# A dispatch kernel bound by its transfers: the tile of 8 tokens moves from the end to the front, the next tile is loaded in four pieces, and the weights come in two loads

## The chip, the core and the metric

The kernel runs on one core of one Trainium2 chip. The metric is the device time of one execution in microseconds (us). Three runs of the kernel before gave 240.56, 240.60 and 241.61 us, a median of 240.6 us. One further execution was taken with the hardware profiler.

## What is computed

Each of 16 x 1024 tokens has a row of 512 float32 numbers and two weights. The output holds, for each token, its row times its first weight and its row times its second weight. The expert indices are an input, but nothing is done with them.

```python
batch, seq, hidden, n_experts = 16, 1024, 512, 8      # k = 2
x_expanded = x[:, :, np.newaxis, :].repeat(k, axis=2)
weights = expert_weights[..., np.newaxis]
return (x_expanded * weights).astype(np.float32)
```

So 33.6 MB of rows are read, 0.13 MB of weights are read, and 67.1 MB are written.

## The kernel before

The 16384 tokens are cut into six tiles over the 128 partitions. A tile of T tokens (per partition) takes T x 128 consecutive tokens, and partition p holds T consecutive ones of them, so that its part of the tile is one unbroken stretch of memory: T x 2 KB of input, T x 4 KB of output. `groups` (L32) gives the sizes: five tiles of 24, and one of 8 at the end. In this text x0 to x5 are the input tiles in the order in which they are loaded, x0.0 is the first piece of x0, and s0, s1, ... are the output stores in their order.

**Weights.** All weights of the core lie in one tile, `w_tile`. Three loads, all issued by SyncE (SP) at the start, fill it: those of the first tile (L53, 192 bytes for each partition), those of the four other tiles of 24 in one load (L54, 4 x 192 bytes for each partition), and those of the last tile (L58, 64 bytes for each partition).

**Input.** `load(i)` (L74) takes one of two input buffers (`x_pool`, 24 tokens each) and issues its loads on ScalarE's (ACT's) queue (L82). The first tile comes in six pieces of 4 tokens (`step`, L80), every other tile in one piece. `load(0)` and `load(1)` are issued at the start; `load(i + 2)` (L119) stands after the products of tile i and reuses its buffer, so it waits until VectorE (DVE) and ACT have read that tile.

**Products.** Each token has k = 2 products, numbered by the weight's column c. Where `c % 3 == 2`, ACT does the product (L100), otherwise DVE (L106): 85 and 171 of them. They are written to one of two output buffers of 12 tokens (`o_pool`, `TO = 12`).

**Output.** After each 12 tokens, or at the tile's end, SP issues one store (L115) of that buffer: ten stores of 12 tokens (6144 KB) and one last store of 8 tokens (4096 KB). A buffer is written again when its store has landed. SP's queue (q1 in the profile) thus carries the three weight loads and then the eleven stores, in this order; ACT's queue (q10) carries the input loads. Nothing but the Python order and the waits on buffers and tiles sets the order of the work.

Of the kernel before, what the change touches and what calls it, by code (L numbers as in the profile page):

```python
# [1 line left out]

# [4 lines left out]


@with_exitstack
def kernel(  # L10
    ctx: ExitStack,
    tc: tile.TileContext,
    x: bass.AP,
    expert_indices: bass.AP,
    expert_weights: bass.AP,
    out: bass.AP,
):
    nc = tc.nc

    batch, seq, hidden = x.shape  # L20
    k = expert_weights.shape[-1]
    P = nc.NUM_PARTITIONS
    ntok = batch * seq
    assert ntok % P == 0
    A_TOTAL = ntok // P

    f32 = mybir.dt.float32
    row = k * hidden
    TX = 24
    TO = 12  # L30

    groups = [[24], [24], [24], [24], [24], [8]]  # L32
    assert sum(sum(g) for g in groups) == A_TOTAL

    xf = x.rearrange("b s h -> (b s) h")
    of = out.rearrange("b s k h -> (b s) (k h)")
    wf = expert_weights.rearrange("b s k -> (b s) k")

    w_pool = ctx.enter_context(tc.tile_pool(name="w_pool", bufs=1))
    x_pool = ctx.enter_context(tc.tile_pool(name="x_pool", bufs=2))  # L40
    o_pool = ctx.enter_context(tc.tile_pool(name="o_pool", bufs=2))

    w_tile = w_pool.tile([P, A_TOTAL * k], f32)

    def rows(of_all, done, T):
        return of_all[done * P : (done + T) * P, :].rearrange(
            "(p a) n -> p (a n)", a=T
        )

    T0 = sum(groups[0])  # L50
    G = len([g for g in groups[1:] if sum(g) == T0])
    head = (1 + G) * T0
    nc.sync.dma_start(out=w_tile[:, : T0 * k], in_=rows(wf, 0, T0))  # L53
    nc.sync.dma_start(  # L54
        out=w_tile[:, T0 * k : head * k].rearrange("p (g n) -> p g n", g=G),
        in_=wf[T0 * P : head * P, :].rearrange("(g p a) n -> p g (a n)", g=G, p=P),
    )
    nc.sync.dma_start(  # L58
        out=w_tile[:, head * k :], in_=rows(wf, head, A_TOTAL - head)
    )  # L60

    tiles = []
    done = 0
    for group in groups:
        T = sum(group)
        a0 = 0
        for n in group:
            tiles.append((done, T, a0, n))
            a0 += n
        done += T  # L70

    loaded = []

    def load(i):  # L74
        if i >= len(tiles):
            return
        done, T, a0, n = tiles[i]
        x_tile = x_pool.tile([P, TX * hidden], f32)
        src = rows(xf, done, T)
        step = TX // 6 if i == 0 else n  # L80
        for at in range(0, n, step):
            nc.scalar.dma_start(  # L82
                out=x_tile[:, at * hidden : (at + step) * hidden],
                in_=src[:, (a0 + at) * hidden : (a0 + at + step) * hidden],
            )
        loaded.append(x_tile)

    for i in range(2):
        load(i)
    for i, (done, T, a0, n) in enumerate(tiles):  # L90
        x_tile = loaded[i]
        outr = rows(of, done, T)
        for t in range(n):
            if t % TO == 0:
                o_tile = o_pool.tile([P, TO * row], f32)
            for kk in range(k):
                c = (done + a0 + t) * k + kk
                o = t % TO * row + kk * hidden
                if c % 3 == 2:
                    nc.scalar.mul(  # L100
                        out=o_tile[:, o : o + hidden],
                        in_=x_tile[:, t * hidden : (t + 1) * hidden],
                        mul=w_tile[:, c : c + 1],
                    )
                    continue
                nc.vector.tensor_scalar(  # L106
                    out=o_tile[:, o : o + hidden],
                    in0=x_tile[:, t * hidden : (t + 1) * hidden],
                    scalar1=w_tile[:, c : c + 1],
                    scalar2=None,  # L110
                    op0=mybir.AluOpType.mult,
                )
            if (t + 1) % TO == 0 or t + 1 == n:
                at = t // TO * TO
                nc.sync.dma_start(  # L115
                    out=outr[:, (a0 + at) * row : (a0 + t + 1) * row],
                    in_=o_tile[:, : (t + 1 - at) * row],
                )
        load(i + 2)  # L119

# [1 line left out]
_INS = ['x', 'expert_indices', 'expert_weights']  # L122
_OUTS = [((16, 1024, 2, 512), 'float32')]


# [23 lines left out]
```

## Time and profile before

| | before |
|---|---|
| median of three runs (lowest to highest) | 240.6 us (240.56 to 241.61) |
| the profiled execution | 240.62 us, with a span of 238.9 us |
| around the span | 1.7 us |
| DVE busy | 69.0 us, 171 products of 480 ns |
| ACT busy | 54.9 us, 85 products of 709 ns and one table load of 1283 ns |
| moved | 100.81 MB in 3986 packets, mean 422 GB/s |

The profiled execution took 240.62 us, as long as the median of the runs. The span goes from the first to the last thing that the profiler records, and 1.7 us lie around it. The core's transfers run on 16 DMA engines. A packet is what one engine moves in one go; here one packet is one partition's part of a transfer, so each large transfer is 128 packets, 8 on each engine. "DMA share" in a row is the mean busy share of the 16 engines in that stretch (it can be over 1.00 in a short stretch, since packets are counted where they start).

### The profile page before, as it was taken

What the parts mean: (1) busy time and instruction counts of PE and PEld (TensorE: products, weight loads), DVE (VectorE), ACT (ScalarE), POOL (GpSimd) and SP (SyncE); (2) the same over time, 40 slices, a digit from 0 to 9 for tenths busy, and PEclk for the clock granted to TensorE, in tenths of its full rate; (3) what the DMA queues carried; (4) which work ended last, traced back from release to release, by engine and by line L of the source; (5) the groups of instructions that cost most, each with busy time, mean ns of one, the idle gap of its engine ahead of it and who ended that gap; (6) DMA issues with size and microseconds to landing.
All of it is one profiled execution on the core that took longest, in us unless ns stands there. A gap on an engine that the chain in (4) does not pass through costs nothing.

```text
span 238.9 us, 364 instructions
## 1 busy us (share of the span) xinstructions
DVE 69.0 (29%) x171; ACT 54.9 (23%) x86; POOL 0.2 (0%) x4
## 2 busy tenths in 40 slices
DVE  0890300004609100190063037003706406415000
ACT  0870300004308000170071034003406106213000
POOL 0000000000000000000000000000000000000000
DMA  6999999999999999999999999999989899999994
GB/s 244 420 443 395 495 395 395 494 428 395 428 494 395 413 494 411 395 446 469 403 411 502 395 420 453 436 411 428 469 379 496 381 428 469 436 411 428 436 439 197
DMA packets 3986, 100.81 MB, mean 422 GB/s; under 512 B 1168, under 2 KB 1168, under 8 KB 1168
## 3 DMA queue, kind: packets, MB, share of 16 engines
q1 hardware_dynamic: 2400, 67.24, 65.2%
q10 hardware_dynamic: 1584, 33.56, 33.1%
q14 instruction: 2, 0.02, 0.0%
HBM read 33.69 MB, written 67.11 MB: 422 GB/s over the span
## 4 chain that ended last, share of the span: by engine, by line
DMA 66%; DVE 13%; another core or an unknown queue 11%; issue 0%; DVEq 0%; SPq 0%
DMA out_dram<-o_tile 54%; DVE o_tile L106 13%; DMA x_tile<-in_x_dram 11%; DVEq L144 0%; DVEq L106 0%; SPq L115 0%
## 5 line engine op out<-in xcount | busy, mean ns | idle before, releaser
L106 DVE TENSOR_SCALAR o_tile<-x_tile,w_tile 128x512 f32<-128x512 f32 x171 | 69.0, 480 | 149.3 <-DMA out_dram<-o_tile 105.3
L100 ACT ACTIVATE o_tile<-x_tile,w_tile 128x512 f32<-128x512 f32 x85 | 53.6, 709 | 155.5 <-DMA out_dram<-o_tile 116.8
L100 ACT ACT_TABLE_LOAD x1 | 1.3, 1283 | 6.7 <-DMA x_tile<-in_x_dram 6.7
L133 POOL MEMSET const-bfloat16-1.0<- 128x1 bf16 x1 | 0.1, 101 | 0.0
L133 POOL MEMSET const-uint8-127<- 128x1 uint8 x1 | 0.1, 101 | 0.0
L133 POOL MEMSET const-float32-0.0<- 128x1 f32 x1 | 0.1, 98 | 0.2 <-issue 0.2
L133 POOL MEMSET const-float32-1.0<- 128x1 f32 x1 | 0.1, 98 | 0.0
## 6 DMA issues: line engine op xcount, KB each, us to landing
out_dram<-o_tile SPq DMA_DIRECT2D x10, 6144.0 KB, 33.6
x_tile<-in_x_dram ACTq DMA_DIRECT2D x4, 6144.0 KB, 43.9
x_tile<-in_x_dram ACTq DMA_DIRECT2D x6, 1024.0 KB, 10.6
out_dram<-o_tile SPq DMA_DIRECT2D x1, 4096.0 KB, 19.5
x_tile<-in_x_dram ACTq DMA_DIRECT2D x1, 2048.0 KB, 24.0
w_tile<-in_expert_weights_dram SPq DMA_DIRECT2D x1, 96.0 KB, 11.1
w_tile<-in_expert_weights_dram SPq DMA_DIRECT2D x1, 24.0 KB, 2.9
w_tile<-in_expert_weights_dram SPq DMA_DIRECT2D x1, 8.0 KB, 13.2
```

The costliest lines, as they stand in the source:

```text
L100: nc.scalar.mul(out=o_tile[:, o : o + hidden], in_=x_tile[:, t * hidden : (t + 1) * hidden], mul=w_tile[:, c : c + 1],)
L106: nc.vector.tensor_scalar(out=o_tile[:, o : o + hidden], in0=x_tile[:, t * hidden : (t + 1) * hidden], scalar1=w_tile[:, c : c + 1], scala ...
L133: nc = _bacc.Bacc("TRN2", target_bir_lowering=False, num_devices=1)
```

## The change

The tile of 8 tokens becomes the first tile, and is loaded in two pieces of 4 tokens. The tile after it (24 tokens) is loaded in four pieces of 6 tokens, and the four others in one piece as before. Each tile's pieces in and out now stand in one list, `plan`. The stores are one of 8 tokens, then ten of 12. With the odd tile in front, the weights of the other five tiles fit one load, so SP issues two weight loads: 64 bytes for each partition, then 5 x 192 bytes.

The core of the diff (the rest writes the same loops in another form: `product` holds the two ways of a product, and the `c % 3` split stays):

```diff
-    TX = 24
-    TO = 12
-    groups = [[24], [24], [24], [24], [24], [8]]
+    plan = [(8, [4, 4], [8]), (24, [6, 6, 6, 6], [12, 12])]
+    plan += [(24, [24], [12, 12])] * 4
...
-    T0 = sum(groups[0])
-    G = len([g for g in groups[1:] if sum(g) == T0])
-    head = (1 + G) * T0
+    T0, T1 = plan[0][0], plan[1][0]
+    G = len(plan) - 1
     nc.sync.dma_start(out=w_tile[:, : T0 * k], in_=rows(wf, 0, T0))
     nc.sync.dma_start(
-        out=w_tile[:, T0 * k : head * k].rearrange("p (g n) -> p g n", g=G),
-        in_=wf[T0 * P : head * P, :].rearrange("(g p a) n -> p g (a n)", g=G, p=P),
-    )
-    nc.sync.dma_start(
-        out=w_tile[:, head * k :], in_=rows(wf, head, A_TOTAL - head)
+        out=w_tile[:, T0 * k :].rearrange("p (g n) -> p g n", g=G),
+        in_=wf[T0 * P :, :].rearrange("(g p a) n -> p g (a n)", g=G, p=P),
     )
...
-        step = TX // 6 if i == 0 else n
-        for at in range(0, n, step):
+        for lo, hi in spans(pieces):
             nc.scalar.dma_start(
-                out=x_tile[:, at * hidden : (at + step) * hidden],
-                in_=src[:, (a0 + at) * hidden : (a0 + at + step) * hidden],
+                out=x_tile[:, lo * hidden : hi * hidden],
+                in_=src[:, lo * hidden : hi * hidden],
             )
...
+    for i, (T, _, outs) in enumerate(plan):
+        dst = rows(of, starts[i], T)
+        for lo, hi in spans(outs):
+            o_tile = o_pool.tile([P, TO * row], f32)
...
+            nc.sync.dma_start(
+                out=dst[:, lo * row : hi * row], in_=o_tile[:, : (hi - lo) * row]
+            )
         load(i + 2)
```

More of the change, by code (lines that the diff above doesn't have):

```diff
@@ L28 @@
     row = k * hidden
-    TX = 24
-    TO = 12
-    groups = [[24], [24], [24], [24], [24], [8]]
-    assert sum(sum(g) for g in groups) == A_TOTAL
+    plan = [(8, [4, 4], [8]), (24, [6, 6, 6, 6], [12, 12])]
+    plan += [(24, [24], [12, 12])] * 4
+    assert sum(T for T, _, _ in plan) == A_TOTAL
+    assert all(sum(i) == T and sum(o) == T for T, i, o in plan)
+    TX = max(T for T, _, _ in plan)
+    TO = max(n for _, _, o in plan for n in o)
     xf = x.rearrange("b s h -> (b s) h")
@@ L48, in rows @@
         )
-    T0 = sum(groups[0])
-    G = len([g for g in groups[1:] if sum(g) == T0])
-    head = (1 + G) * T0
+    T0, T1 = plan[0][0], plan[1][0]
+    G = len(plan) - 1
+    assert all(T == T1 for T, _, _ in plan[1:])
     nc.sync.dma_start(out=w_tile[:, : T0 * k], in_=rows(wf, 0, T0))
     nc.sync.dma_start(
-        out=w_tile[:, T0 * k : head * k].rearrange("p (g n) -> p g n", g=G),
-        in_=wf[T0 * P : head * P, :].rearrange("(g p a) n -> p g (a n)", g=G, p=P),
-    )
-    nc.sync.dma_start(
-        out=w_tile[:, head * k :], in_=rows(wf, head, A_TOTAL - head)
-    )
@@ L62, with spans @@
[L62 to L70, printed above, removed]
+        out=w_tile[:, T0 * k :].rearrange("p (g n) -> p g n", g=G),
+        in_=wf[T0 * P :, :].rearrange("(g p a) n -> p g (a n)", g=G, p=P),
+    )
+    def spans(sizes):
+        at = 0
+        for n in sizes:
+            yield at, at + n
+            at += n
+    starts = [lo for lo, _ in spans([T for T, _, _ in plan])]
@@ L72 @@
     loaded = []
     def load(i):
-        if i >= len(tiles):
+        if i >= len(plan):
             return
-        done, T, a0, n = tiles[i]
+        T, pieces, _ = plan[i]
         x_tile = x_pool.tile([P, TX * hidden], f32)
-        src = rows(xf, done, T)
-        step = TX // 6 if i == 0 else n
-        for at in range(0, n, step):
+        src = rows(xf, starts[i], T)
+        for lo, hi in spans(pieces):
             nc.scalar.dma_start(
-                out=x_tile[:, at * hidden : (at + step) * hidden],
-                in_=src[:, (a0 + at) * hidden : (a0 + at + step) * hidden],
+                out=x_tile[:, lo * hidden : hi * hidden],
+                in_=src[:, lo * hidden : hi * hidden],
@@ L85, in load @@
             )
         loaded.append(x_tile)
[L88 to L103, printed above, removed]
-                    )
[L105 to L118, printed above, removed]
@@ new lines, in product @@
+    def product(o_tile, o, x_tile, t, c):
+        if c % 3 == 2:
+            nc.scalar.mul(
+                out=o_tile[:, o : o + hidden],
+                in_=x_tile[:, t * hidden : (t + 1) * hidden],
+                mul=w_tile[:, c : c + 1],
+            )
+        else:
+            nc.vector.tensor_scalar(
+                out=o_tile[:, o : o + hidden],
+                in0=x_tile[:, t * hidden : (t + 1) * hidden],
+                scalar1=w_tile[:, c : c + 1],
+                scalar2=None,
+                op0=mybir.AluOpType.mult,
+            )
@@ new lines @@
+    load(0)
+    load(1)
+    for i, (T, _, outs) in enumerate(plan):
+        dst = rows(of, starts[i], T)
+        for lo, hi in spans(outs):
+            o_tile = o_pool.tile([P, TO * row], f32)
+            for t in range(lo, hi):
+                for kk in range(k):
+                    product(
+                        o_tile,
+                        (t - lo) * row + kk * hidden,
+                        loaded[i],
+                        t,
+                        (starts[i] + t) * k + kk,
+                    )
+            nc.sync.dma_start(
+                out=dst[:, lo * row : hi * row], in_=o_tile[:, : (hi - lo) * row]
+            )
```

## The prediction

> **What bounds the kernel now.** I read the page's slices and queues first. "DMA" is the busy share of the 16 DMA engines in tenths, in 40 slices of 6.0 us; below it is what they moved.
>
> ```profile
> DMA  6999999999999999999999999999989899999994
> GB/s 244 420 443 395 495 395 395 494 428 395 428 494 395 413 494 411 395 446 469 403 411 502 395 420 453 436 411 428 469 379 496 381 428 469 436 411 428 436 439 197
> ...
> q1 hardware_dynamic: 2400, 67.24, 65.2%
> q10 hardware_dynamic: 1584, 33.56, 33.1%
> ```
>
> The engines are full in all slices but the first and the last: 65.2% + 33.1% = 98.3% of 16 engines' span. DVE (29%) and ACT (23%) are idle mostly because they wait for transfers. So I cut the span into stretches (columns: DVE, ACT and POOL busy, clock, DMA share, GB/s):
>
> ```profile
> 3.00:14.00 11.00, 6.82 (x17) 6.61 (x10) 0.00 (x0) 1.00 1.02 416
> 14.00:16.90 2.90, 2.88 (x8) 1.75 (x4) 0.00 (x0) 1.00 1.03 362
> 16.90:40.00 23.10, 3.51 (x9) 3.26 (x6) 0.00 (x0) 1.00 1.01 432
> 40.00:120.00 80.00, 19.27 (x48) 15.03 (x24) 0.00 (x0) 1.00 1.00 434
> 150.00:193.00 43.00, 12.85 (x32) 10.02 (x16) 0.00 (x0) 1.00 1.00 432
> 193.00:235.00 42.00, 10.87 (x27) 8.18 (x13) 0.00 (x0) 1.00 0.99 430
> 235.00:238.90 3.90, 0.00 (x0) 0.00 (x0) 0.00 (x0) 1.00 0.24 101
> ```
>
> From 40 to 120 us the rate is 434 GB/s, whether loads run beside stores or, after 193 us, stores run alone (430). All 100.81 MB at 434 would be 232.3 us; the span has 6.6 us more. By rows: the start to 3.0 us (about 0.25 MB moved there) loses 2.4; the stretch with 8 KB load packets, 3 to 14 us at 416, loses 11 x (1 - 416/434) = 0.46; the 2.9 us in which the first store joins lose 2.9 x (1 - 362/434) = 0.48; the last 3.9 us at 101 GB/s lose 3.0; the rest is 0.3. By the trace's packet records the 16 engines stop between 235.8 and 237.6 us, on average at 236.4, and 1.3 us follow the last packet. That is all a new order of transfers could win.
>
> The start in order of time:
>
> ```profile
> 5.85 2.46 DVE L106 TENSOR_SCALAR o_tile<-x_tile,w_tile 128x512 f32<-128x512 f32 x6 [5.85 <-DMA x_tile<-in_x_dram]
> 6.70 1.28 ACT L100 ACT_TABLE_LOAD   x1 [6.70 <-DMA x_tile<-in_x_dram]
> 8.64 2.07 DVE L106 TENSOR_SCALAR o_tile<-x_tile,w_tile 128x512 f32<-128x512 f32 x5 [0.33 <-DMA x_tile<-in_x_dram]
> 11.23 2.07 DVE L106 TENSOR_SCALAR o_tile<-x_tile,w_tile 128x512 f32<-128x512 f32 x5 [0.52 <-DMA x_tile<-in_x_dram]
> 13.38 17.16 SPq L115 DMA_DIRECT2D out_dram<-o_tile  x2
> ```
>
> A piece of 1024 KB lands every 2.6 us, and the first store is issued at 13.38. In the packet records its first packet moves at 17.0; the loads issued beside running stores at 127.86 and 171.63 first move at 131.6 and 175.4. So 3.6 to 3.8 us pass from issue to first packet on a busy core.
>
> **The change part by part.**
>
> *Fewer, larger packets.* From the packet records 8 KB takes 0.309 us, 16 KB 0.611, 48 KB 1.815; 12 KB lies at about 0.46. Loads in small pieces were 768 x 0.309 + 128 x 0.611 = 315.5 us of engine time and become 256 x 0.309 + 512 x 0.46 = 314.6: 0.9 over 16 engines, -0.06 us. Bytes, 171 + 85 products and the store packets (1280 of 48 KB, 128 of 32 KB) stay.
>
> *Earlier first store.* x0 is complete with its second piece at 8.64. Of its 16 products DVE has 11 (6 before 8.64, 5 after, 2.07 us), ACT 5 (the table load no longer stands behind seven load issues; three products of 0.71 us after 8.64). So s0 is issued at about 10.8 instead of 13.38. This is worth nothing by itself: the engines are full with loads until then, and the same bytes are still to move.
>
> *Weights.* The 64-byte load takes the place of the 192-byte one in front and lands well before 5.85 (before: 2.9 us after issue). The second has 640 small packets, as many as L54 and L58 had together; these had landed at 1.63 + 13.2 = 14.8, L54 alone (512 packets) at 1.16 + 11.1 = 12.3. So 12.3 to 14.8. s0 stands behind it on SP's queue: its first packet at about 14.5 (10.8 + 3.7, the same). SP issues one load less (0.5 us, hidden). Zero.
>
> ```profile
> w_tile<-in_expert_weights_dram SPq DMA_DIRECT2D x1, 96.0 KB, 11.1
> w_tile<-in_expert_weights_dram SPq DMA_DIRECT2D x1, 24.0 KB, 2.9
> w_tile<-in_expert_weights_dram SPq DMA_DIRECT2D x1, 8.0 KB, 13.2
> ```
>
> The Trainium skill (DMA: Bandwidth & Descriptors, "Anatomy of one DMA — SWDGE (gpsimd) path") gives each transfer a fixed cost of about 2.0 us, stated for the gpsimd path. With 23 transfers in place of 25 it would make 4.0 us less, 236.6, if none of it were hidden; the 8.0 KB row, which lands while the engines are full, shows that it is hidden here.
>
> *New wait on ACT's queue.* As the changed kernel is built, ACT's sixth product (the second tile's first) stands ahead of the load of x2 and waits for x1.0 and the second weights; x2's load is queued behind it, and the DMA engines wait for that. x1.0 lands at 8.64 + 1.5 x 2.6 = 12.5, the weights by 14.8, so x2 starts to move by 14.8 + 0.8 (that product) + 3.8 (issue to first packet) = 19.4. The cover is x1, which alone lasts to 8.64 + 6 x 2.6 = 24.2, and s0's 4096 KB (9.7 us at 434): together 33.9. Without s0 it would still be 4.8 us. Zero; past 33.9 each us costs one.
>
> *Does SP's queue run dry?* With loads behind it this loses no engine time, but a store queue that starts again may cost a dip like the 0.48. The queues alternate packet by packet, each engine 8 packets a transfer. From 14.5 s0 and x1 (0.46 + 1.21 us a pair) take 13.4 us, so s0 ends at 27.9. x1.1 had 2 to 3 packets left at 14.5 and lands by about 18.5; 8 DVE products more, s1 issued at 22, moving by 25.7, before s0 is done. s1 then runs beside x1.2 and x1.3 (0.46 + 1.82 a pair) to about 46; x1.3 lands at 47, 3.3 us of products, s2 issued at 51, moving at 54.5. So SP's queue is empty once more, from 46 to 54.5, beside x2's 48 KB packets. No row of before has a store start beside those. Bounds: 0, by the load queue that starts again at 131.6 and 175.4 without a visible dip (432 in 150 to 193), and 0.48. I take 0.2, nearer to the first, since the packet sizes are those.
>
> *End.* After the last load only stores run, each waiting for a buffer: landing to next issue 6.5 us (16 DVE products of 6.43) and 3.7 to its first packet, 10.2, against 14.5 for the other buffer's 6144 KB at 434. Cover 4.3 us, as now. As no small tile is left, the store-only stretch begins earlier; I estimate some 23 us earlier, and 430 against 432 makes 0.1. The engines' stops, 1.25 us from mean to last, may be closer or wider: -1.2 to +0.6, taken as 0, since every engine has the same packets.
>
> *Sum:* 238.9 - 0.06 + 0.2 + 0.1 = 239.1 of span, plus 1.7: 240.8. The profiled execution (240.62) equals the median, so nothing is added.
>
> **Rivals.**
>
> *Slower: the store queue starts afresh several times.* If s0 moves already at 12.5, x1.1 has 6 to 7 packets left, lands at 23.8, and s1 moves only at 31, after s0 has ended at 25.9; s2 as above, and s3 too if x2 lands over 2.6 us later than I have it. Three starts at 0.48 are 1.44: 242.1; with the deeper start of small packets, 0.63 by the packet records, 242.5. It decides when s0's first packet is ahead of about 13.5 and the price holds beside large packets. For it: the 362 row. Against: no dip at 131.6 or 175.4.
>
> *Faster: the joining loss goes.* If s0 joins beside 12 KB packets without the 362 row (-0.48), half of the 416 loss goes (-0.23) and the engines stop half as far apart (-0.6), the span is 237.6: 239.3. For it: the loss sits where packets are smallest. Against: three parts must all come.
>
> *It does not do what it says:* s0 waits behind 640 weight packets, its first packet is at 17 as before, and nothing moves: 240.6.
>
> **How the numbers follow.** Within 0.5% is about what a measurement of this kernel can tell from no change (1.2 us, 239.4 to 241.8). My forecast has 0.60, its own range 239.7 to 241.7; the idle rival 0.05; both are "same": 0.65. The restarts have 0.21, all slower; the joining loss 0.14, faster. The range takes in both rivals' prices, 239.3 to 242.5, leaving out about 0.15.
>
> **What would show it.** First store issued near 10.8; second weights landing at 12.3 to 14.8; DMA share at 1.0 from 3 us to the end; a start of s2 near 54 beside a rate that stays at 430 or more. Wrong would be: a slice below 9 in the middle, a stretch below 400 after 20 us, or a start above 3 us to full rate.

## The result, and the profile after

The changed kernel took 242.02 us (median of 22 runs, 240.81 to 246.77), the kernel before 240.66 (22 runs, 240.53 to 241.61): a ratio of 1.0062 (95% interval 1.0048 to 1.0075), so it is slower by 0.6%. Its runs also scatter by 6 us (3.3 without the highest), where those of before lie within 1.1. The profiled execution took 242.59 us with a span of 240.8, somewhat above the median. (The ratios in this document leave out runs more than 1.5% above the fastest of their kernel; where a kernel's runs fall into two groups, that leaves out the upper one, and the text gives both.)

The page's slices and queues after, to be laid beside those of before:

```profile
DMA  6999999999999999999999999999999999999993
GB/s 223 424 400 461 441 437 441 412 416 351 449 465 392 442 465 400 433 474 400 416 475 416 408 482 416 400 490 408 400 490 416 400 474 433 400 457 441 408 441 147
...
q1 hardware_dynamic: 2384, 67.24, 64.8%
q10 hardware_dynamic: 1440, 33.56, 33.2%
```

The engines are as full as before: 98.0% of the span against 98.3%. But the tenth slice moved only 351 GB/s with its DMA digit at 9. The stretches say where (same columns as before: DVE, ACT, POOL, clock, DMA share, GB/s):

```profile
3.00:14.00 11.00, 4.54 (x11) 4.57 (x6) 0.00 (x0) 1.00 1.02 415
14.00:17.00 3.00, 0.00 (x0) 0.00 (x0) 0.00 (x0) 1.00 1.07 398
17.00:48.00 31.00, 9.77 (x24) 7.68 (x12) 0.00 (x0) 1.00 1.01 434
52.00:57.00 5.00, 0.15 (x1) 0.00 (x0) 0.00 (x0) 1.00 0.99 334
57.00:120.00 63.00, 17.09 (x43) 14.30 (x23) 0.00 (x0) 1.00 1.00 432
120.00:235.00 115.00, 34.32 (x86) 25.79 (x42) 0.00 (x0) 1.00 1.01 436
```

From 52 to 57 us the share is 0.99 and the rate 334: the engines are not idle, their packets take longer. Measured against the 434 GB/s of before, the loss is 5 x (1 - 334/434) = 1.15 us. In the packet records a 48 KB packet takes 1.815 us; 11 of 1792 took over 1.9 us before, together 0.21 us for each engine, and 34 after, 1.35 us.

By the packet records the profiled spans differ by 1.87 us in this way: the engines start 0.22 later on average (2.57 against 2.35), their slow packets cost 0.94 more in sum over the load and store packets (2.28 against 1.34 us an engine), the last engine stops 1.52 instead of 1.19 us after the mean, and 1.67 instead of 1.30 us follow the last packet. 0.22 + 0.94 + 0.33 + 0.37 = 1.86. (The records do not name the engine; packets are put in a row by one's end and the next's start.)

Of the 1.35 us, 1.08 lie between 52 and 56 us: 18 load packets of x2, of which sixteen, as many as there are engines, are under way at once near 55.6 us. After 60 us the packets over 1.9 us cost only 0.03 us an engine, against 0.17 in the kernel before. So in this run it is mainly one delay that all engines share. How far apart the engines are shows in another record: each transfer closes with one packet of 4 bytes for each engine. At the last five stores the first and the last of these packets lie 2.4 to 2.6 us apart, against 1.8 to 1.9 before.

The start and the middle in order of time:

```profile
17.20 3.26 DVE L91 TENSOR_SCALAR o_tile<-x_tile,w_tile 128x512 f32<-128x512 f32 x8 [6.08 <-DMA w_tile<-in_expert_weights_dram]
17.25 0.33 ACTq L77 DMA_DIRECT2D x_tile<-in_x_dram  x1
21.45 3.26 DVE L91 TENSOR_SCALAR o_tile<-x_tile,w_tile 128x512 f32<-128x512 f32 x8 [1.00 <-DMA x_tile<-in_x_dram]
35.48 3.26 DVE L91 TENSOR_SCALAR o_tile<-x_tile,w_tile 128x512 f32<-128x512 f32 x8 [10.77 <-DMA x_tile<-in_x_dram]
48.90 3.26 DVE L91 TENSOR_SCALAR o_tile<-x_tile,w_tile 128x512 f32<-128x512 f32 x8 [10.16 <-DMA x_tile<-in_x_dram]
```

The four pieces of x1 release DVE at 17.2 (held by the weights), 21.45, 35.48 and 48.90. s0 was issued at 11.20, s1 at 24.77, s2 at 52.22. In the packet records s0 first moves at 14.7 and ends at 30.2, s1 ends at 48.5, and s2 first moves at 56.8: SP's queue is empty from 48.5 to 56.8, and the shared delay lies just ahead of its new start.

### The profile page after: what moved, and what is told of

It is laid out like the page before. It is cut to its first block, busy times and chain, and to the rows that moved or that the text cites. A ratio compares the mean times of both kernels' runs of the same rounds, so it can differ in the third digit from the quotient of the medians.

```text
span 240.8 us, 366 instructions
## 1 busy us (share of the span) xinstructions
DVE 69.0 (29%) x171; ACT 54.9 (23%) x86; POOL 0.2 (0%) x4
## 4 chain that ended last, share of the span: by engine, by line
DMA 76%; DVE 12%; ACTq 1%; issue 0%; DVEq 0%; SPq 0%
DMA out_dram<-o_tile 58%; DMA x_tile<-in_x_dram 19%; DVE o_tile L91 12%; ACTq L77 1%; DVEq L142 0%; DVEq L91 0%; SPq L114 0%
## 6 DMA issues: line engine op xcount, KB each, us to landing
x_tile<-in_x_dram ACTq DMA_DIRECT2D x4, 1536.0 KB, 25.8
```

## The experiments

Three theories stood against each other at first. A: the new start of the empty store queue costs the time. B: the front costs it (the 64-byte weights first, one load of 640 small packets). C: the end costs it (a last store of 12 tokens). A fourth was added after the first runs (the pieces of 6, 6 and 12, the uncut tile, the smaller last store, and the kernel before with its first tile in pieces of 6). D: the second tile's small load packets, run beside stores, bring DMA engines out of step with each other (some finish their part of a transfer later than the others), and these then lose time. All kernels were timed against the kernel before, whose median was 240.58 to 240.67 us each time.

**Cutting the second tile differently.**

```diff
-    plan = [(8, [4, 4], [8]), (24, [6, 6, 6, 6], [12, 12])]
+    plan = [(8, [4, 4], [8]), (24, [6, 6, 12], [12, 12])]
```

> The changed kernel with the second tile loaded in three pieces of 6, 6 and 12 tokens instead of four of 6. Theory A (the store queue runs empty and its new start beside loads costs about 1.1 us of every DMA engine): the last piece now has 8 packets of 24 KB an engine in place of 16 of 12 KB, needs fewer turns beside the first two stores and lands before 40 us; the third store is issued near 43 us, before the second has ended near 48, so the queue does not run empty: 240.6 to 241.2 us, and no stretch below 400 GB/s after 20 us. Theory B (the front: the 64-byte weights first and 640 small packets ahead of the first store) and theory C (the end: the last store is 12 tokens instead of 8 and the engines stop further apart): nothing of theirs is touched, 242.0 us within 0.4.

Measured: 252.36 us (250.64 to 255.03), ratio 1.0477 (1.0436 to 1.0517). All three theories missed. The store queue is never empty between the first and the third store (s1 first moves at 31.1 while s0 ends at 32.9, s2 at 60.2 while s1 ends at 62.0), as theory A wanted it, and yet the kernel loses 12 us. Its stretches:

```profile
57.00:104.00 47.00, 8.10 (x21) 6.79 (x11) 0.00 (x0) 1.00 0.99 413
104.00:106.00 2.00, 2.00 (x6) 2.00 (x5) 0.00 (x0) 1.00 0.91 393
106.00:108.00 2.00, 2.00 (x6) 1.23 (x3) 0.00 (x0) 1.00 0.23 98
108.00:120.00 12.00, 0.75 (x2) 0.00 (x0) 0.00 (x0) 1.00 0.93 344
```

Here 176 of the 1792 packets of 48 KB are slow, 5.84 us for each engine. In the packet records three engines are slow again and again, about every 4 us, by 0.3 to 1.2 us at a time, from 32 to 113 us; the others far less often. A store has landed only when its last engine is done: the 4-byte packets of s2 show thirteen engines done by 90.0 us and three at 100.1 to 101.7, and DVE goes on at 102.3. So the products of the next stores wait for the laggards, and at 106 us the other engines have nothing left: share 0.23. Not all of the 5.84 us is theirs. Some 3.2 of it lie from 108 to 120 and from 156 to 164 us, where up to 15 and 13 slow packets are under way at once. At the end most engines stop at 245.1, the last at 251.6.

```diff
-    plan = [(8, [4, 4], [8]), (24, [6, 6, 6, 6], [12, 12])]
+    plan = [(8, [4, 4], [8]), (24, [24], [12, 12])]
```

> The changed kernel with the second tile loaded in one piece of 24 tokens. Theory A (new start of an empty store queue): the first store (8 packets of 32 KB an engine) alternates with 48 KB load packets and lasts to about 39 us; the second tile lands near 29, the second store is issued near 36 and the third near 42, so the queue has at most a short gap before the second store: 240.6 to 241.4 us. Theory B (front) and theory C (end): 242.0 us within 0.4.

Measured: 240.81 us (240.03 to 242.06), ratio 1.0009 (0.9994 to 1.0024). Undoing the four pieces alone gives the time back. The tile in front, the two weight loads and the end are all still there, so B and C fall. A expected it, and D, formed later, fits it as well: the 640 weight packets take until 24 us here (the last 128 from 8 us on, one for each load packet), s0 first moves at 22.9, and x1 has by then all but landed (23.9). A delay that engines share is there in this kernel too, just ahead of s0: thirteen load packets are slow at once at 21.3 us. It falls into the first of these stretches:

```profile
20.00:24.00 4.00, 0.00 (x0) 0.00 (x0) 0.00 (x0) 1.00 0.90 334
24.00:60.00 36.00, 12.85 (x32) 10.02 (x16) 0.00 (x0) 1.00 1.00 431
60.00:235.00 175.00, 51.39 (x128) 40.09 (x64) 0.00 (x0) 1.00 1.01 435
```

The edit also moves s0 behind x1, so by itself it does not tell the pieces from the pieces beside stores. In the kernel before, the uncut x1 (25.8 to 54.9 us) runs beside the first two stores.

```diff
-    plan = [(8, [4, 4], [8]), (24, [6, 6, 6, 6], [12, 12])]
+    plan = [(8, [4, 4], [8]), (24, [4] * 6, [12, 12])]
```

> The changed kernel with the second tile loaded in six pieces of 4 tokens (8 KB packets, those of the kernel before) instead of four of 6. The last piece lands near 48 us again and the store queue is empty from about 44 to 56 us. Theory A: 242.0 us within 0.5. Theory D, with 12 KB packets as the cause: 240.6 to 241.2 us.

Measured: 242.86 us (241.08 to 243.47), ratio 1.0074 (1.0051 to 1.0098). So 12 KB as a size is not special. The median lies above the ranges of both theories (A's ends at 242.5), and A's mechanism was not there: in the profiled run s1 ended at 54.7 and s2 first moved at 52.8, so the queue was not empty, against my arithmetic.

```diff
-    plan = [(8, [4, 4], [8]), (24, [6, 6, 6, 6], [12, 12])]
+    plan = [(8, [4, 4], [8]), (24, [12, 12], [12, 12])]
```

> The changed kernel with the second tile loaded in two pieces of 12 tokens (24 KB packets). The second piece lands near 35 us and the third store is issued near 42, before the second ends, so the store queue stays filled. Theory A: 240.6 to 241.2 us. Theory D, if it is the 24 KB packets beside stores that put engines out of step in the run with pieces of 6, 6 and 12 (252.4 us): well above 242 us.

Measured: median 241.25 us, ratio 1.0023 (1.0010 to 1.0035); nine of eleven runs lie from 240.69 to 242.06, two at 252.55 and 252.56. The median is just above A's range. D's "well above 242" came out in two runs only, which took as long as those with pieces of 6, 6 and 12.

**Keeping the store queue filled, with the pieces as they are.**

```diff
-    plan = [(8, [4, 4], [8]), (24, [6, 6, 6, 6], [12, 12])]
+    plan = [(8, [4, 4], [8]), (24, [6, 6, 6, 6], [12, 6, 6])]
```

> The changed kernel with the second tile stored in pieces of 12, 6 and 6 tokens instead of 12 and 12; its loads stay in four pieces of 6. The third store then needs only the third piece (landed at 35.4 us in the changed kernel's trace) and is issued near 39 us, before the second store ends at 48.5, so the store queue does not run empty. Theory A (an empty store queue pays about 1.1 us of all engines when it starts again): 240.6 to 241.2 us. Theory D (some DMA engines fall behind the others after 12 KB load packets have run beside stores, and the stores wait for the slowest engine): unchanged, 242.0 us within 0.5.

Measured: 242.09 us (241.53 to 244.01), ratio 1.0074 (1.0050 to 1.0099). The third store first moves at 46.5, before the second ends at 48.1. The queue is not empty, and nothing is won in the median, so A falls. The slow packets are there all the same (52 over 1.9 us, 1.21 us an engine; 14 load packets at once near 53.7 us), though the stretch around them loses less, 5 x (1 - 388/434) = 0.53 us:

```profile
30.00:46.00 16.00, 3.26 (x8) 2.56 (x4) 0.00 (x0) 1.00 1.01 432
46.00:50.00 4.00, 0.00 (x0) 0.00 (x0) 0.00 (x0) 1.00 1.05 427
50.00:55.00 5.00, 3.26 (x8) 2.56 (x4) 0.00 (x0) 1.00 1.02 388
55.00:120.00 65.00, 19.28 (x48) 15.03 (x24) 0.00 (x0) 1.00 1.00 434
```

**The front and the end.**

```diff
     nc.sync.dma_start(
-        out=w_tile[:, T0 * k :].rearrange("p (g n) -> p g n", g=G),
-        in_=wf[T0 * P :, :].rearrange("(g p a) n -> p g (a n)", g=G, p=P),
+        out=w_tile[:, T0 * k : (T0 + T1) * k], in_=rows(wf, T0, T1)
+    )
+    nc.sync.dma_start(
+        out=w_tile[:, (T0 + T1) * k :].rearrange("p (g n) -> p g n", g=G - 1),
+        in_=wf[(T0 + T1) * P :, :].rearrange("(g p a) n -> p g (a n)", g=G - 1, p=P),
     )
```

> The changed kernel with its weights in three loads (those of the first tile, of the second tile, and of the other four) instead of two. The second tile's weights land by about 7 us instead of 17, so its first products and the load of the third tile come some 5 us earlier; as many small packets stand ahead of the first store. Theory B (the single load of 640 small packets holds things up): 240.6 to 241.2 us. Theories A and D: 242.0 us within 0.5, since the third store still waits for the fourth piece near 49 us.

Measured: median 242.39 us, ratio 1.0056 (1.0033 to 1.0078); five of seven runs from 240.9 to 243.2, two at 252.74 and 253.71. B is not the cause. The store queue was not empty here either, against the expectation: s2 was issued at 43.1, and first moved at 60.5 while s1 ended at 62.2. So this run speaks against A as well.

```diff
-    plan += [(24, [24], [12, 12])] * 4
+    plan += [(24, [24], [12, 12])] * 3 + [(24, [24], [12, 8, 4])]
```

> The changed kernel with the last tile stored in pieces of 12, 8 and 4 tokens instead of 12 and 12, so that the last store is smaller than that of the kernel before (8). Theory C (the end): the engines stop closer together, 240.8 to 241.4 us. Theory A (new start of an empty store queue near 52 us) and theory B (front): 242.0 us within 0.4.

Measured: 242.17 us (241.70 to 242.94), ratio 1.0063 (1.0049 to 1.0078). The last store is a third as large, and nothing changes. C falls.

**The pieces, but no store beside them.** The first store is held until the pieces have landed:

```diff
+            if (i, lo) == (0, 0):
+                held = (dst, o_tile, hi)
+                continue
+            if (i, lo) == (1, 0):
+                dst0, o0, n0 = held
+                nc.vector.tensor_scalar(
+                    out=o0[:, n0 * row - 1 : n0 * row],
+                    in0=o_tile[:, (hi - lo) * row - 1 : (hi - lo) * row],
+                    scalar1=1.0, scalar2=None, op0=mybir.AluOpType.mult,
+                )
+                nc.sync.dma_start(
+                    out=dst0[:, : n0 * row], in_=o0[:, : n0 * row]
+                )
             nc.sync.dma_start(
                 out=dst[:, lo * row : hi * row], in_=o_tile[:, : (hi - lo) * row]
             )
```

> The changed kernel with its first store held back: one more DVE instruction copies one number per partition from the second output buffer into the first (so one number in each partition's part of the first tile is replaced), and the first store waits for it. It is issued near 24 us instead of 11, when the four pieces of the second tile have landed, so no 12 KB load packet runs beside a store; the pieces, the weights and the tile order stay. Theory D (small load packets beside stores put DMA engines out of step, and those then lose time): 240.5 to 241.2 us. A theory that the front itself (tile order, weights, start) costs the time: 242.0 us within 0.5.

Measured: 241.52 us (241.22 to 245.02), ratio 1.0034 (1.0021 to 1.0047): between the two expectations. x1 ended at 23.5 us and s0 first moved at 26.9. About half of the loss goes.

The same with the second tile in pieces of 6, 6 and 12:

> The same held-back first store (one number in each partition's part of the first tile is replaced) with the second tile in pieces of 6, 6 and 12, which took 252.4 us with the early store. Theory D: the pieces have landed before the first store runs, so 240.5 to 241.5 us. If these pieces or the front put the engines out of step by themselves, without a store beside them: 250 us or more.

Measured: 241.59 us (240.86 to 243.24), ratio 1.0045 (1.0027 to 1.0063), against 252.36 with the early store. The 11 us are gone with one wait *added*, while pieces, weights, order and end stayed. The stretches of the run with the late store:

```profile
30.00:60.00 30.00, 6.42 (x16) 5.01 (x8) 0.00 (x0) 1.00 0.98 422
60.00:120.00 60.00, 19.28 (x48) 15.04 (x24) 0.00 (x0) 1.00 1.01 436
120.00:176.00 56.00, 12.85 (x32) 10.02 (x16) 0.00 (x0) 1.00 0.98 424
```

No stretch falls to a share of 0.23; by the packet records the engines' excess over 1.815 us for each 48 KB packet adds up to 0.62 us after 60 us, against 5.22 with the early store.

**The pieces alone, in the kernel before.** Three edits of one expression (L80):

```diff
-        step = TX // 6 if i == 0 else n
+        step = TX // 6 if i == 0 else 6 if i == 1 else n     # second tile in pieces of 6
+        step = TX // 6 if i == 0 else 12 if i == 1 else n    # second tile in pieces of 12
+        step = TX // 4 if i == 0 else n                      # first tile in pieces of 6
```

> The kernel before with one part of the change alone: its second tile is loaded in four pieces of 6 tokens instead of one of 24. The tile of 8 stays at the end, the weights stay in three loads. Its 12 KB load packets run beside the first two stores. Theory D: 241.4 to 243 us. A theory that the tile of 8 in front or the two weight loads cost the time: 240.5 to 240.9 us.

Measured: four of six runs from 250.74 to 253.77, two at 242.69 and 243.02 (median of all 251.26; ratio of the two low runs 1.0089, 1.0067 to 1.0111). More than expected: this part alone does more harm than the whole change. Its stretches show the two ways in which time goes:

```profile
40.00:60.00 20.00, 6.43 (x16) 5.01 (x8) 0.00 (x0) 1.00 1.00 431
60.00:130.00 70.00, 12.85 (x32) 10.02 (x16) 0.00 (x0) 1.00 1.00 400
130.00:140.00 10.00, 6.43 (x16) 5.01 (x8) 0.00 (x0) 1.00 0.93 378
140.00:150.00 10.00, 0.00 (x0) 0.00 (x0) 0.00 (x0) 1.00 0.99 369
```

From 60 to 130 us the share is 1.00 and the rate only 400: full engines, slow packets (on one engine a store packet takes 0.53 to 0.72 us more than 1.815 every 4.25 us or so, fourteen times in a row). Then the share falls, since the next store waits for the slowest: the 4-byte packets of one store lie up to 15.4 us apart here.

> The kernel before with its second tile loaded in two pieces of 12 tokens (24 KB packets) beside the first two stores. Theory D: between the kernel before and the one with pieces of 6, 240.8 to 242 us, with single runs far above (two of eleven runs of the changed kernel with pieces of 12 were at 252.6). A theory that the tile order or the weights cost the time: 240.5 to 240.9 us with no run far above.

Measured: 242.26 us (241.22 to 243.00), ratio 1.0063 (1.0039 to 1.0088), just above the expected range; no run far above.

> The kernel before with only its first tile cut differently: four pieces of 6 tokens instead of six of 4. It keeps the three weight loads and the tile of 8 at the end. Theory A: the store queue stays fed (second store issued near 25 us, the first lasts beyond 40), 240.4 to 240.8 us. Theory B and theory C: the same 240.4 to 240.8. A theory that pieces of 12 KB are bad as such: 242 us.

Measured: 241.20 us (240.74 to 242.55), ratio 1.0029 (1.0017 to 1.0041). No expectation was right. These 12 KB pieces ran beside weight packets and no store (s0 first moved at 38.1, behind the weights, instead of 17.0), and the kernel still lost 0.3%; whether by the pieces or by the later store is not separated.

## Why the prediction was right or wrong, point by point

**The direction of the most likely case was wrong, the range held.** 240.8 and "same" had 0.65; the kernel came out slower, 242.02, inside 239.3 to 242.5 and just under the price that the rival of new starts had been given (242.1 to 242.5), but not by its mechanism. That the range held is luck: what moved the time stands in no term of the sum and in no rival. One of the signs named for being wrong did show, a stretch below 400 GB/s after 20 us: 334 from 52 to 57.

**Right.** An earlier first store is worth nothing where the engines are full: s0 was issued at 11.20 (forecast 10.8), moved at 14.7 (14.5), and bought no time. From 120 us to 235 the rate is 436 GB/s, the store-only end included, with no gap. The wait on ACT's queue for x2 is hidden (x2 was issued at 17.25, and x1 lasted to 48). The queue is empty before s2: issued at 52.2 (51), moving at 56.8 (54.5).

**The step that failed: "Fewer, larger packets", -0.06 us.** It priced the cut of the second tile by the packets' own durations, as if these stayed the same whatever runs beside them. Undoing the cut takes the median from 242.02 to 240.81, so the term is about +1.2 us; in the kernel before the cut alone costs +2.2 us in the low group and over 10 in the high one. In the runs near 252 us, what grows is the time of the 48 KB packets that follow, for which the sum had no term (5.84 and 7.18 us an engine). "Every engine has the same packets" was true and not enough: there a few engines were slow repeatedly. In the changed kernel itself, single engines that are slow again and again (theory D) are not seen: its profile has the one shared delay at 52 to 56 us, 0.03 us an engine after 60, and at the end a spread somewhat wider than before. Nor do slow 48 KB packets order the kernels of the low group: the profiled run of 241.25 us (two pieces) has 0.04 us of them an engine, the one of 240.78 (uncut) 0.61, the one of 241.53 (stores of 12, 6 and 6) 1.21. So which part of the trace makes the +1.2 us stays open.

**The price of a new start, 0.2 us, was too low for this trace and is not the cause.** 1.15 us were lost just there in the profiled run. But with the queue empty from 48.3 to 55.6 in the run with the smaller last store, the same place lost 5 x (1 - 364/434) = 0.8:

```profile
52.00:57.00 5.00, 0.00 (x0) 0.00 (x0) 0.00 (x0) 1.00 0.89 364
```

and with the queue filled 0.53 were still lost near there and the median stayed (242.09). An empty queue marks the place in one trace; filling it wins no time.

**Weights: too early.** I had them at 12.3 to 14.8, by those of before; they landed at 17.2. They stand against x1's 12 KB packets now, and from about 6 us on a small packet waits for a load packet each time (the last 384, 24 for each engine, take 10.7 us, 0.45 us each; a 12 KB packet takes 0.46). The Trainium skill (DMA: Bandwidth & Descriptors, "Queues, rings and completion order") has each engine go round its queues packet by packet, and the traces agree: the same 640 packets ended at 16.6 us beside 12 KB loads and at 24.0 beside 48 KB ones. The delay cost nothing that shows: with the second tile's weights in a load of their own, its first products began at 12.7 us instead of 17.2, and the kernel was no faster (242.39).

**What is shown and what is not.** Shown: the four pieces carry the loss (undone, it goes; alone, they make it and more), and for the worst case it takes the stores beside the pieces (held back, 11 of 12 us go). Not shown: by which path the pieces cost the changed kernel its 1.2 us, since single engines that are slow for long are seen clearly only in the profiles near 252 us; why the packets take longer; and why the kernels whose pieces have no store beside them still lose 0.3 to 0.45%. Each kernel has one profiled execution, and the runs of the changed kernel scatter by more than the loss. Also open is what decides between the two groups of runs (near 242 and near 252) of one kernel.

No version beat the kernel before; the best, with the second tile uncut, equals it (1.0009, 0.9994 to 1.0024).

## What to carry to other kernels

In this kernel, with all DMA engines full, an earlier first store and an earlier small tile won nothing, and cutting a load lost time. Look at the rate beside the share: 334 or 400 GB/s at a share of 0.99 or 1.00 were slow packets, not missing work. Before cutting a load that runs beside stores, ask who waits for its pieces; here the earlier pieces bought no time, and the kernels with this load uncut were the fastest. When one place in a single trace looks guilty, take it away before believing it: here the empty queue could be filled without any gain. And look for a slow stretch in the fast kernels too: the one with the tile uncut has 334 GB/s from 20 to 24 us and is as fast as the kernel before.

## What was not expected of the hardware

- The same 48 KB packet took 1.815 us in most cases, and 1.9 to 3.5 us in others; in one profiled run of 252.3 us (the kernel before with its second tile in pieces of 6), 215 slow packets of 1664 made up 7.18 us an engine, with the same bytes.
- One kernel, one core, two groups of runs: 240.69 to 242.06 and 252.55 to 252.56 (second tile in two pieces).
- One engine that lags is paid by all: with the share at 0.23 from 106 to 108 us, the others waited for a store whose last three engines were done 10 us after the other thirteen.
- All engines can have a slow load packet at once: sixteen were under way together near 55.6 us in the changed kernel, thirteen at 21.3 us in the kernel with the tile uncut.
- A wait added in front of the first store made a kernel faster, 252.36 to 241.59 us.
